# Sums of squares moved from GpSimd to TensorE, and three additions from GpSimd to VectorE, at the ends of layers

## The chip, the cores and the metric

The kernel runs on one core of a Trainium2 chip. The metric is the device time of one execution in microseconds; lower is better. Engines are named as in the profile: PE is TensorE (PEld its weight loads), DVE is VectorE, ACT is ScalarE, POOL is GpSimd, SP issues DMAs.

## The reference

The reference runs two layers of a streaming encoder on two streams, a prompt of 256 frames and 64 further frames of a running stream. The kernel handles both at once as T = 320 tokens, with D = 1024 features.

```python
for layer in range(DEPTH):                                   # DEPTH = 2
    h = rmsnorm(x, norm_mix_pre[layer])
    mix = mamba2_mixer(h, ...) if layer < N_A else mla_attend(h, ...)
    x = x + rmsnorm(mix, norm_mix_post[layer])
    f = conv_ffn(rmsnorm(x, norm_ffn_pre[layer]), ...)
    x = x + rmsnorm(f, norm_ffn_post[layer])
    if layer == N_A - 1:                                     # after the first layer
        latent, key = mla_shared_kv(x, ...)                  # starts with rmsnorm(x, kv_norm_in)
```

`rmsnorm(x, g)` is `x * rsqrt(mean(x*x) + 1e-6) * g`, the mean being over the features of a token. Four times the stream x goes through a pre-norm into a large product: at the start (Mamba input projection), at the first FFN, at the attention layer (latent, key and query projections share one sum of squares), and at the second FFN.

## The kernel before

**Layout.** x lies in SBUF as eight blocks of 128 features by 320 tokens: features on partitions, so the mean over features is a sum over partitions and over blocks. Every product with weights is done in three f32r matmuls (`mm3`): high part of the weight by high part of x (`wh`, `xgh`), `wh` by the low part `xgl`, and the weight's low part `wl` by `xgh`. ACT makes the high parts, DVE the low ones (POOL in part of the attention). Weights stream from HBM through `wr` (3 buffers) into `wh` and `wl` (4 each); an 'early' pool (`eh`, `el`) keeps a few units of the next stage.

**Scheduling.** The program is written in Python order, and a planner with its own costs sets the order on each engine; DVE and ACT between the last output block of a layer and the end of `enter` keep the written order (`self.region`). `after()` adds orderings by hand; `behind` in `outer_part` puts products behind a given PE instruction.

**End of a layer and entry of the next.** `post()` scales the eight output blocks into `y` (pool `yp`, opened by `open_y`, closed by `self.yst.close()`) and sums their squares. `late_rstd()` makes the reciprocal root of the output's mean square (`pow` on POOL, `rk`), spreads it over the partitions by PE into a PSUM tile `pr`, and returns that tile as `r`. Then `enter()` goes over the eight blocks k: `y_k *= r` (L442, DVE); `x_k += y_k` (L446, DVE, but POOL for k = 3, 5, 7); `xgh_k` (ACT, L411; for k = 0 DVE, L444); the low part `xgl` of the block before (DVE, L418 or L421); and the square of the block before (ACT, L433), which POOL adds to `xacc` (L434). At the start of the program `enter` runs with `boundary=False`, on x from the DMA.

**Products on x before its norm.** The pre-norm's root is a factor for each token, so products run on x itself (times the gain) and are scaled afterwards. `outer()` multiplies k-block by k-block into 6 PSUM tiles (4 at the start): k = 0 to 5, then `rstd_of(xacc)`, which is `toksum` (three PE matmuls of `xacc` with a column of ones, one for each 128 tokens, into a `pr` tile, L352), `mean` (DVE, `nwv`, L346) and `newton` (POOL `pow`, `rk`, L340); then k = 6 behind the sums; then `rstd_sb` (spread over partitions by PE, L359, copy by ACT to `xr`, L378); then k = 7. What follows the products (`conv` with its DVE scaling `ext`, `normalized` with `xn` on POOL) needs `xr`. In `mla()` the sums of `xacc` and of the latent's squares `kacc` go into one `pr` tile, between products k = 4 and k = 5 of the query part.

**PSUM pools.** `self.psum(**...)` closes one set of PSUM pools and opens another. Sets: `PSM = dict(m=4, x=3, r=1)` (mixer), `PSF` and `PSL = dict(m=7, r=1)` (FFN and the attention's entry), `PSA = dict(m=5, x=3)` (attention). `pr()` takes a buffer of `r` where the set has one, else of `x`.

Of the kernel before, what the change touches and what calls it, by code (L numbers as in the profile page):

```python
# [11 lines left out]
AF = mybir.ActivationFunctionType  # L12
ALU = mybir.AluOpType
# [3 lines left out]
P = 128  # L17
T = 320
TP = 256
TS = 64  # L20
D = 1024
KD = 8
NBF = 22
EPS = 1e-6
# [21 lines left out]
PSF = dict(m=7, r=1)  # L46
PSL = dict(m=7, r=1)
# [39 lines left out]
class Kern:  # L87
# [252 lines left out]
        self.nw_end = self.nc.gpsimd.tensor_tensor(out=r, in0=v, in1=self.half[:, 0:v.shape[1]], op=ALU.pow).ins  # L340
        return r

    def mean(self, src, dim, pool):

        v = self.t(pool, [P, 3], "nwv", bufs=3)
        self.nc.vector.tensor_scalar(v, src, 1.0 / dim, EPS, op0=ALU.mult, op1=ALU.add)  # L346
        return v

# [47 lines left out]
            self.high_ahead(HIGH[b])  # L396
        return ps

    def enter(self, xgp, sp, tag, g=None, boundary=True):


        nc = self.nc
        tt, act = nc.vector.tensor_tensor, nc.scalar.activation
        r = self.late_rstd() if boundary else None
        xh = self.t(xgp, [P, KD, T], "xgh", F32R, bufs=1)
        xl = self.t(xgp, [P, KD, T], "xgl", F32R, bufs=1)
        acc = self.t(sp, [P, T], "xacc", bufs=1)
        self.xhigh = []

        def high(k):  # L410
            i = act(out=xh[:, k, :], in_=self.x[:, k, :], func=AF.Copy, scale=self.v(g, k) if g and k else 1.0)  # L411
            if boundary:
                self.xhigh.append(i.ins)

        def low(k):
            h = xh[:, k, :].bitcast(F32)
            if g and k:
                i = nc.vector.scalar_tensor_tensor(out=xl[:, k, :], in0=self.x[:, k, :], scalar=self.v(g, k), in1=h,  # L418
                                                   op0=ALU.mult, op1=ALU.subtract)
            else:  # L420
                i = tt(out=xl[:, k, :], in0=self.x[:, k, :], in1=h, op=ALU.subtract)  # L421
            self.low_end = i.ins
            if boundary and k in AHEAD:
                self.gate = i.ins
                if self.lows:
                    self.lows.pop(0)()

        def square(k):
            if k == 0:
                act(out=acc, in_=self.x[:, k, :], func=AF.Square)  # L430
                return
            s = self.t(sp, [P, T], tag, bufs=2)
            act(out=s, in_=self.x[:, k, :], func=AF.Square)  # L433
            nc.gpsimd.tensor_tensor(out=acc, in0=acc, in1=s, op=ALU.add)  # L434

        with self.region if boundary else ExitStack():
            for k in range(KD + 1):
                if k < KD:
                    xk = self.x[:, k, :]
                    if boundary:  # L440
                        yk = self.y[:, k, :]
                        tt(out=yk, in0=yk, in1=r, op=ALU.mult)  # L442
                        if k == 0:
                            tt(out=xh[:, k, :], in0=xk, in1=yk, op=ALU.add)  # L444
                        e = nc.gpsimd if k in (3, 5, 7) else nc.vector
                        e.tensor_tensor(out=xk, in0=xk, in1=yk, op=ALU.add)  # L446
                        if k:
                            high(k)
                        else:
                            low(k)  # L450
                    else:
                        high(k)
                        low(k)
                if boundary and k > 1:
                    low(k - 1)
                if k:
                    square(k - 1)
        if boundary:
            self.ends.pop(0)
        return xh, xl, acc  # L460

    def normalized(self, xgp, sp, g, rstd):

# [110 lines left out]
    def outer_part(self, ps, ks, xh, xl, behind=None, turned=False):  # L574

        w = {}
        ks = list(ks)
        if ks[0] == 0:
            ks.pop(0)
            wh, wl = self.nextw()  # L580
            for j, (wt, xt) in enumerate(((wh, xh), (wl, xh), (wh, xl))):
                for b, p in enumerate(ps):
                    self.nc.tensor.matmul(p[:, :T], wt[:, b * 128:b * 128 + 128], xt[:, 0, :], start=j == 0, stop=False)
        for k, b in [(k, b) for b in range(len(ps)) for k in ks] if turned else [(k, b) for k in ks for b in range(len(ps))]:
            if k not in w:
                w[k] = self.nextw()
            s = slice(b * 128, b * 128 + 128)
            self.mm3(ps[b][:, :T], w[k][0][:, s], w[k][1][:, s], xh[:, k, :], xl[:, k, :], k == 0, k == KD - 1, behind)

    def outer(self, nblk, xh, xl, xacc, pool):  # L590

        ps = [self.pm() for _ in range(nblk)]
        a, b = OUT
        self.outer_part(ps, range(a), xh, xl)
        r = self.rstd_of(xacc, D, pool)
        self.gate = self.nw_end
        self.outer_part(ps, range(a, b), xh, xl, self.pe_end)
        r = self.rstd_sb(r, pool, "xr")
        self.outer_part(ps, range(b, KD), xh, xl, self.pe_end)
        self.xhigh = []  # L600
        return ps, r
# [96 lines left out]
    def ssm(self):  # L698
# [3 lines left out]
        with ExitStack() as st:  # L702
# [5 lines left out]
            with ExitStack() as s2:  # L708
# [4 lines left out]
                with ExitStack() as s3:  # L713
                    xtp = self.pool(s3, "xg0")
                    dp = self.pool(s3, "dtp")
                    nc.scalar.dma_start(out=self.vec[:, 0:8], in_=a["vec"][:, 0:8])
                    for k in range(KD):
                        r = self.raw[k] = self.t(dp, [P, 512], "w0", bufs=KD)
                        nc.sync.dma_start(out=r, in_=a["w_in_k"][k])
                        nc.sync.dma_start(out=self.x[:, k, :], in_=a["x"][:, k * T:(k + 1) * T])  # L720
                    nc.sync.dma_start(out=self.con, in_=a["con"][:, 0:CON["cos"][0]])
                    nc.sync.dma_start(out=self.vec[:, 8:], in_=a["vec"][:, 8:])
                    self.qd = KD
                    xh, xl, xacc = self.enter(xtp, dp, "xsq", "mix_pre0", False)
                    ps, rstd = self.outer(4, xh, xl, xacc, dp)
                    self.bt, self.ct, self.xs = {}, {}, {}
                    dt2 = self.ssm_dt(ps[0], rstd, sp, dp)
                    for i in range(1, 4):
                        self.ssm_conv(i - 1, ps[i], rstd, sp)
                    xnh, xnl, steps = self.normalized(xgp, dp, "mix_pre0", rstd)  # L730
                    szs = {0: self.t(sp, [P, 4, T], "sz", bufs=2)}
                    for i in range(3, 3 + RAW0):
                        if i == 6:
                            self.exps = self.burst = []
                            self.ssm_dt2(dt2, sp, dp)
                        p = self.block(xh, xl)
                        if i < 6:
                            self.ssm_conv(i, p, rstd, sp)
                        else:
                            nc.vector.tensor_tensor(out=szs[0][:, i - 6, :], in0=p[:, :T], in1=rstd, op=ALU.mult)  # L740
                        while len(steps) > (6, 5, 3, 1, 0)[i - 3]:
                            steps.pop(0)()
                    xh, xl = xnh, xnl
# [291 lines left out]
    def ffn(self, i):  # L1035
        nc, a = self.nc, self.a
        with ExitStack() as st:
# [3 lines left out]
            with ExitStack() as s2:  # L1041
                xgp = self.pool(s2, f"xgf{i}")
                sp = self.pool(s2, f"fs{i}")
                fsave = self.t(sp, [P, 44, 2, 2], "fsave")
                xh, xl, xacc = self.enter(xgp, sp, "xsq", f"ffn_pre{i}")
                self.yst.close()
                self.psum(**(PSF, PSL)[i])
                ps, rstd = self.outer(6, xh, xl, xacc, sp)
                self.est.close()
                self.table(AF.Gelu_apprx_tanh)  # L1050
                xnh, xnl, steps = self.normalized(xgp, sp, f"ffn_pre{i}", rstd)
# [39 lines left out]
    def mla(self):  # L1091
        nc, a = self.nc, self.a
        tt, ts, stt = nc.vector.tensor_tensor, nc.vector.tensor_scalar, nc.vector.scalar_tensor_tensor
        with ExitStack() as st:
# [10 lines left out]
            with ExitStack() as s2:  # L1105
# [3 lines left out]
                oldt = self.t(sp, [P, 2, 256], "oldt")  # L1109
                nc.sync.dma_start(out=old, in_=a["old"].rearrange("p (a b) -> p a b", a=3))  # L1110
                nc.sync.dma_start(out=oldt, in_=a["oldt"].rearrange("p (a b) -> p a b", a=2))
                xh, xl, xacc = self.enter(xgp, sp, "xsq")
                self.yst.close()
                self.psum(**PSF)
                u = self.t(kp, [P, 2, T], "u")
                kacc = self.t(sp, [P, T], "kacc")
# [16 lines left out]
                self.outer_part(ps, range(4, 5), xh, xl)  # L1133


                pt = self.pr()
                self.toksum(xacc, pt)
                self.toksum(kacc, pt, 3)
                vs = self.t(sp, [P, 6], "vs")
                ex = self.t(sp, [P, 3], "ex")  # L1140
                ts(vs[:, 0:3], pt[:, 0:3], 1.0 / D, EPS, op0=ALU.mult, op1=ALU.add)
                ts(ex, vs[:, 0:3], EPS, None, op0=ALU.mult)
                stt(out=vs[:, 3:6], in0=pt[:, 3:6], scalar=1.0 / 256, in1=ex, op0=ALU.mult, op1=ALU.add)
                self.outer_part(ps, range(5, 7), xh, xl, self.pe_end)
                rr = self.newton(vs, sp, "rr")
                r2 = self.rstd_sb(rr[:, 3:6], sp, "xk")
                xr = self.rstd_sb(rr[:, 0:3], sp, "xr", self.pm())
# [410 lines left out]
```

## Time and profile before

| | us |
|---|---|
| median of 3 runs | 983.34 (982.84 to 984.02) |
| profiled execution | 985.59 |
| its span in the trace | 983.8 |

| engine | busy us (share of the span) | instructions |
|---|---|---|
| PE | 960.0 (98%) | 6602 |
| PEld | 932.7 (95%) | 6602 |
| DVE | 738.8 (75%) | 1348 |
| ACT | 614.0 (62%) | 1247 |
| POOL | 353.5 (36%) | 560 |

The mean granted clock of PE was 0.992. How to read the rows of a timeline: start and length in us, the engine, the line of the kernel, the operation, the tile written and the tiles read, the shape; in brackets the time for which the engine stood idle before it, and what it had been waiting for. A row `x6` merges six instructions. Matmuls are pipelined and their ends are modelled, so the distance between starts is the time that a matmul takes up on PE. The four entries lie at 0 to 44 us (start), 264 to 300 (first FFN), 505 to 535 (attention) and 729 to 758 (second FFN).

### The profile page before, as it was taken

The numbers are of one execution on the slowest core, as the hardware profiler recorded it, in microseconds if no ns is written. First come the engines' busy times: TensorE is split into PE (matmuls) and PEld (weight loads), VectorE is DVE, ScalarE is ACT, GpSimd is POOL, SyncE is SP. The second block draws the span as 40 slices with busy tenths as digits, with TensorE's granted clock in tenths as the row PEclk, the third lists the DMA queues.
The fourth block names the chain that finished last, engine by engine and source line by source line (L and its number), as shares of the span: only waits on it lengthen the run. The fifth ranks groups of instructions, "written<-read, shape, count | busy, mean of one in ns | idle before, by whom it ended". The sixth has DMA issues, their size and how long they took to land.

```text
span 983.8 us, 17990 instructions
## 1 busy us (share of the span) xinstructions
PE 960.0 (98%) x6602; PEld 932.7 (95%) x6602; DVE 738.8 (75%) x1348; ACT 614.0 (62%) x1247; POOL 353.5 (36%) x560
## 2 busy tenths in 40 slices
PE   8799999999999999999999999999999999999997
PEld 8799999989989999999999899999999999999996
DVE  7989889975579998765547898885638999775432
ACT  7568988644556787654444677764645678665331
POOL 5822411000056875420017766520005777441000
PEclk9899999999999999999999999999999999999999
DMA  7465646443334545455631222233534454445541
GB/s 256 143 196 181 202 134 204 139 134 118 103 119 131 171 150 172 150 181 165 195 112 37 81 73 76 57 97 108 172 107 127 129 174 151 151 145 147 153 118 54
DMA packets 45945, 135.58 MB, mean 138 GB/s; under 512 B 5408, under 2 KB 10144, under 8 KB 45856
## 3 DMA queue, kind: packets, MB, share of 16 engines
q1 hardware_dynamic: 45712, 134.42, 43.9%
q8 instruction: 52, 0.85, 0.4%
q14 instruction: 37, 0.30, 0.1%
q10 hardware_dynamic: 144, 0.00, 0.0%
HBM read 130.29 MB, written 4.11 MB: 137 GB/s over the span
## 4 chain that ended last, share of the span: by engine, by line
PE 83%; DVE 9%; POOL 3%; ACT 2%; issue 2%; DMA 0%; SPq 0%; POOLq 0%; DVEq 0%; ACTq 0%
PE pm L284 47%; PE pm L285 23%; PE px L284 3%; PE px L285 1%; PE px L987 1%; PE px L970 1%; PE pr L352 1%; POOL xacc L434 1%; DVE wl L329 1%; PE px L978 1%; ACT wh L327 1%; POOL xn L470 1%; DVE xnl L331 1%; DVE cv L670 1%; PE px L953 1%
## 5 line engine op out<-in xcount | busy, mean ns | idle before, releaser
L329 DVE TENSOR_TENSOR wl<-wr,wh 128x1024 fp32r<-128x1024 f32 (+2 forms) x204 | 242.9, 1191 | 108.7 <-ACT wh L327 107.6
L327 ACT ACTIVATE wh<-wr 128x1024 fp32r<-128x1024 f32 (+4 forms) x235 | 227.7, 971 | 149.1 <-PE pm L284 131.5
L284 PE MATMUL pm<-xnh,wh 128*128 128x320 f32 x768 | 239.2, 312 | 0.2 <-DVE ext L660 0.2
L284 PE MATMUL pm<-xnl,wh 128*128 128x320 f32 x768 | 239.3, 312 | 0.0
L285 PE MATMUL pm<-xnh,wl 128*128 128x320 f32 x768 | 238.2, 310 | 0.0
L284 PEld LDWEIGHTS pm<-xnl,wh 128*128 128x128 f32 x768 | 144.2, 188 | 3.0 <-issue 3.0
L285 PEld LDWEIGHTS pm<-xnh,wl 128*128 128x128 f32 x768 | 144.2, 188 | 1.7 <-issue 1.7
L284 PEld LDWEIGHTS pm<-xnh,wh 128*128 128x128 f32 x768 | 144.2, 188 | 1.5 <-issue 0.7
L285 PE MATMUL pm<-ah,wl 128*128 128x320 f32 x424 | 131.3, 310 | 0.0
L284 PE MATMUL pm<-al,wh 128*128 128x320 f32 x424 | 131.2, 310 | 0.0
L284 PE MATMUL pm<-ah,wh 128*128 128x320 f32 x424 | 131.1, 310 | 0.0
L670 DVE SCALAR_TENSOR_TENSOR cv<-ext,vec,cv 128x322 f32<-128x322 f32 x176 | 98.2, 569 | 6.1 <-ACT cv L668 3.6
L664 POOL COPY fsave<-ext 128x2 f32<-128x2 f32 x88 | 71.1, 808 | 50.5 <-ACT ext L658 46.9
L340 POOL TENSOR_TENSOR rk<-nwl,half 128x3 f32<-128x3 f32 x4 | 3.4, 851 | 216.5 <-DVE nwl L391 216.5
L284 PEld LDWEIGHTS pm<-ah,wh 128*128 128x128 f32 x424 | 79.5, 188 | 1.0 <-issue 1.0
L285 PEld LDWEIGHTS pm<-ah,wl 128*128 128x128 f32 x424 | 79.6, 188 | 0.2 <-issue 0.2
L284 PEld LDWEIGHTS pm<-al,wh 128*128 128x128 f32 x424 | 79.6, 188 | 0.0
L284 PE MATMUL pm<-xgh,wh 128*128 128x320 f32 x236 | 68.6, 320 | 7.2 <-ACT xs L689 5.9
L285 PE MATMUL pm<-xgh,wl 128*128 128x320 f32 x236 | 74.2, 317 | 0.7 <-DVE wl L331 0.7
L284 PE MATMUL pm<-xgl,wh 128*128 128x320 f32 x236 | 74.1, 317 | 0.5 <-DVE xgl L418 0.5
L668 ACT ACTIVATE cv<-ext,vec 128x322 f32<-128x322 f32 x88 | 57.0, 653 | 15.1 <-POOL ext L655 9.7
L329 POOL TENSOR_TENSOR wl<-wr,wh 128x512 fp32r<-128x512 f32 (+2 forms) x31 | 43.7, 1424 | 25.2 <-ACT wh L327 22.7
(384 smaller groups left out, 2196.5 us busy)
## 6 DMA issues: line engine op xcount, KB each, us to landing
wr<-w_up SPq DMA_DIRECT2D x76, 512.0 KB, 3.3
wr<-w_in SPq DMA_DIRECT2D x37, 512.0 KB, 3.9
wr<-w_dn SPq DMA_DIRECT2D x32, 512.0 KB, 3.6
wr<-w_out SPq DMA_DIRECT2D x16, 512.0 KB, 3.4
wr<-w_o SPq DMA_DIRECT2D x16, 512.0 KB, 3.3
wr<-w_up_k SPq DMA_DIRECT2D x16, 384.0 KB, 3.4
wr<-w_dn SPq DMA_DIRECT2D x16, 384.0 KB, 3.2
dc<-acd SPq DMA_DIRECT2D x8, 512.0 KB, 6.0
```

The lines of the kernel that those rows point to most:

```text
L284: for i in (mm(out, wh, xh, start=first, stop=False), mm(out, wh, xl, start=False, stop=False), mm(out, wl, xh, start=False, stop=last)):
L285: mm(out, wl, xh, start=False, stop=last)):
L327: self.high_ins = nc.scalar.activation(out=hdst, in_=src, func=AF.Copy).ins
L329: return lambda: e.tensor_tensor(out=ldst, in0=src, in1=hdst.bitcast(F32), op=ALU.subtract)
L331: return lambda: nc.vector.scalar_tensor_tensor(out=ldst, in0=src, scalar=scale, in1=hdst.bitcast(F32), op0=ALU.mult, op1=ALU.subtract)
L352: i = self.nc.tensor.matmul(ps[:, o + b:o + b + 1], acc[:, l0:l0 + 128], self.ones[:, 0:1], start=True, stop=True)
L434: nc.gpsimd.tensor_tensor(out=acc, in0=acc, in1=s, op=ALU.add)
L470: nc.gpsimd.tensor_tensor(out=xn, in0=self.x[:, k, :], in1=rstd, op=ALU.mult)
L664: nc.gpsimd.tensor_copy(out=rows_out[:, 0, :], in_=ext[:, TP:TP + m])
L668: nc.scalar.activation(out=c, in_=ext[:, 0:n], func=AF.Identity, scale=w(0), bias=b)
L670: nc.vector.scalar_tensor_tensor(out=c, in0=ext[:, i:i + n], scalar=w(i), in1=c, op0=ALU.mult, op1=ALU.add)
L953: nc.tensor.transpose(xt_[:n, j * 128:j * 128 + 128], xs[j][:, l0:l0 + n], self.ident)
```

## The change

- `square(k)`: ACT still squares each block of x, but at an end of a layer it writes the square over the old output block `y[:, k, :]` (whose product with `r` has been added to x by then), and at the start of the program into one of eight `xsq` buffers instead of two. `xacc` and POOL's additions into it are gone.
- Each square gets a set of three PE matmuls with the column of ones (each block's set accumulates into the same three columns of one `pr` tile, `sums_tile`). The sets wait in a list, `self.sums`. `outer_part` issues the next one ahead of the weights of k while more than `KD - k + 1` are left (so block k - 2 ahead of product k); `result()`, returned by `enter` in place of `acc`, issues what is left and then `mean`.
- `outer` and `mla` call that function where they called `rstd_of(xacc)` and `toksum(xacc)`. The matmuls of the sets do not set `pe_end`, so k = 6 stands behind an older instruction than before.
- `x_k += y_k` runs on DVE for every k.
- In `ffn` and `mla`, `self.yst.close()` comes after the products instead of before them.

```diff
-    def mean(self, src, dim, pool):
+    def mean(self, src, dim, pool, v=None):
-        v = self.t(pool, [P, 3], "nwv", bufs=3)
+        v = self.t(pool, [P, 3], "nwv", bufs=3) if v is None else v
...
-    def enter(self, xgp, sp, tag, g=None, boundary=True):
+    def enter(self, xgp, sp, tag, g=None, boundary=True, mean=None):
...
-        acc = self.t(sp, [P, T], "xacc", bufs=1)
+        self.sums = []
...
         def square(k):
-            if k == 0:
-                act(out=acc, in_=self.x[:, k, :], func=AF.Square)
-                return
-            s = self.t(sp, [P, T], tag, bufs=2)
+            s = self.y[:, k, :] if boundary else self.t(sp, [P, T], tag, bufs=KD)
             act(out=s, in_=self.x[:, k, :], func=AF.Square)
-            nc.gpsimd.tensor_tensor(out=acc, in0=acc, in1=s, op=ALU.add)
+
+            def add():
+                if k == 0:
+                    self.sums_tile = self.pr()
+                sums = self.sums_tile
+                for b, l0 in enumerate(TOK):
+                    nc.tensor.matmul(sums[:, b:b + 1], s[:, l0:l0 + 128], self.ones[:, 0:1], start=k == b == 0, stop=k == KD - 1 and b == 2)
+
+            self.sums.append(add)
...
-                        e = nc.gpsimd if k in (3, 5, 7) else nc.vector
-                        e.tensor_tensor(out=xk, in0=xk, in1=yk, op=ALU.add)
+                        tt(out=xk, in0=xk, in1=yk, op=ALU.add)
...
-        return xh, xl, acc
+
+        def result():
+            while self.sums:
+                self.sums.pop(0)()
+            return self.mean(self.sums_tile[:, 0:3], D, sp, mean)
+
+        return xh, xl, result
...
             if k not in w:                                   # outer_part
+                if not turned and len(self.sums) > KD - k + 1:
+                    self.sums.pop(0)()
                 w[k] = self.nextw()
...
-    def outer(self, nblk, xh, xl, xacc, pool):
+    def outer(self, nblk, xh, xl, xv, pool):
...
-        r = self.rstd_of(xacc, D, pool)
+        r = self.newton(xv(), pool, "rk")
...                                                          # ffn
-                self.yst.close()
                 self.psum(**(PSF, PSL)[i])
-                ps, rstd = self.outer(6, xh, xl, xacc, sp)
+                ps, rstd = self.outer(6, xh, xl, xv, sp)
+                self.yst.close()
                 self.est.close()
...                                                          # mla
-                xh, xl, xacc = self.enter(xgp, sp, "xsq")
-                self.yst.close()
+                vs = self.t(sp, [P, 6], "vs")
+                xh, xl, xv = self.enter(xgp, sp, "xsq", mean=vs[:, 0:3])
                 self.psum(**PSF)
...
-                pt = self.pr()
-                self.toksum(xacc, pt)
+                xv()
+                pt = self.sums_tile
                 self.toksum(kacc, pt, 3)
-                vs = self.t(sp, [P, 6], "vs")
...
-                ts(vs[:, 0:3], pt[:, 0:3], 1.0 / D, EPS, op0=ALU.mult, op1=ALU.add)
...
                 self.outer_part(ps, range(5, 7), xh, xl, self.pe_end)
+                self.yst.close()
```

More of the change, by code (lines that the diff above doesn't have):

```diff
@@ L723, in ssm @@
                     self.qd = KD
-                    xh, xl, xacc = self.enter(xtp, dp, "xsq", "mix_pre0", False)
-                    ps, rstd = self.outer(4, xh, xl, xacc, dp)
+                    xh, xl, xv = self.enter(xtp, dp, "xsq", "mix_pre0", False)
+                    ps, rstd = self.outer(4, xh, xl, xv, dp)
                     self.bt, self.ct, self.xs = {}, {}, {}
@@ L1044, in ffn @@
                 fsave = self.t(sp, [P, 44, 2, 2], "fsave")
-                xh, xl, xacc = self.enter(xgp, sp, "xsq", f"ffn_pre{i}")
+                xh, xl, xv = self.enter(xgp, sp, "xsq", f"ffn_pre{i}")
+                self.psum(**(PSF, PSL)[i])
+                ps, rstd = self.outer(6, xh, xl, xv, sp)
                 self.yst.close()
-                self.psum(**(PSF, PSL)[i])
-                ps, rstd = self.outer(6, xh, xl, xacc, sp)
                 self.est.close()
```

## The prediction

> **What bounds the kernel now.** I read the busy times and the chain of waits first, then the busy time by stage, then the timeline of TensorE (PE) around the four places that the change touches, and last the rows of the tiles it drops.
>
> ```profile
> PE 960.0 (98%) x6602; PEld 932.7 (95%) x6602; DVE 738.8 (75%) x1348; ACT 614.0 (62%) x1247; POOL 353.5 (36%) x560
> ...
> PE 83%; DVE 9%; POOL 3%; ACT 2%; issue 2%; DMA 0%; SPq 0%; POOLq 0%; DVEq 0%; ACTq 0%
> ```
> ```profile
> 45.00:240.00 195.00, 195.00 (x1409) 182.95 (x1409) 170.03 (x286) 143.31 (x273) 37.79 (x44) 0.99 0.53 165
> 285.90:293.30 7.40, 5.45 (x25) 4.95 (x25) 3.17 (x4) 3.54 (x7) 2.94 (x3) 0.77 0.60 201
> 325.00:505.00 180.00, 180.00 (x1230) 180.00 (x1229) 129.20 (x216) 111.46 (x219) 64.88 (x143) 1.00 0.54 165
> 729.00:760.00 31.00, 30.15 (x213) 28.85 (x212) 20.68 (x37) 15.29 (x30) 13.04 (x13) 1.00 0.26 84
> 760.00:967.00 207.00, 207.00 (x1413) 207.00 (x1412) 147.20 (x252) 122.61 (x236) 81.62 (x178) 1.00 0.46 141
> ```
>
> By the second line of the page, PE makes up 83% of the chain that ends last, POOL 3%. In the rows by stage the columns are the stretch, its length, then PE, weight loads, DVE, ACT, POOL, the granted clock and the DMA. In three long stretches (582 of 983.8 us) PE is busy for every microsecond. Busy matmul time can overstate, but the products in it start every 0.15 us without a break (next fence). So outside the short holes, a microsecond of PE work that is added is a microsecond of time, and only a hole can absorb it. The second row is such a hole, with the clock down to 0.77; the fourth, the last of the four places, holds hardly any: 0.85 us idle.
>
> **What a set of three token sums costs.** Both kernels sum over partitions by f32 matmuls with a column of ones, one for each block of 128 tokens, and each is issued as two, so a set is six weight loads and six matmuls. The rows are one set among dense products, and one before k = 6:
>
> ```profile
> 263.99 0.31 PE L285 MATMUL pm<-ah,wl 128*128 128x320 f32 x1
> 264.13 0.72 PE L352 MATMUL pr<-ones,yacc 128*128 128x1 f32 x6
> 264.72 0.39 PE L284 MATMUL pm<-ah,wh 128*128 128x320 f32 x1
> 264.95 0.31 PE L284 MATMUL pm<-al,wh 128*128 128x320 f32 x1
> ```
> ```profile
> 293.35 0.72 PE L352 MATMUL pr<-ones,xacc 128*128 128x1 f32 x6
> 293.94 0.39 PE L284 MATMUL pm<-xgh,wh 128*128 128x320 f32 x1
> ```
>
> Starts are read, not durations. A set pushes the next product back by 0.59 us both times (264.72 - 264.13; 293.94 - 293.35), and the product behind it starts 0.23 instead of 0.15 us later: 0.59 for sets in a row, 0.67 for a lone one. Before, each place issues one set on the finished `xacc`; after, one set for each of eight blocks, so seven more at each of four places: 28 sets, 168 matmuls. Between 28 x 0.59 = 16.5 and 28 x 0.67 = 18.8 us I take 0.60, nearer the low end, since the last two to four sets of a place stand in a row by the order of the code, and more will if the first ones wait for the last `y` (a rival, below): 4.2 us a place, 16.8 us in all.
>
> The Trainium skill, page "TensorE: Matmul & The Clock Gate", section "Back-to-back issue gap", puts a matmul of 1 to 64 columns at about 25 ns, and its section "Step-by-step: what each phase is for" has the weight loads pulled ahead under running matmuls; by these two my estimate of a set is 6 x 25 = 150 ns, and the 28 sets would be 4.2 us instead of 16.8. The rows do not agree: 0.59 us for six is 98 ns a pair, since a matmul of one column leaves nothing to hide the next load behind.
>
> **What leaves POOL, and what comes to DVE.**
>
> ```profile
> L434 POOL TENSOR_TENSOR xacc<-xacc,xsq x28: 877/1010/1632, 7.9 to 751.7; 128x320 f32<-128x320 f32 x28
> ```
> ```profile
> L446 DVE TENSOR_TENSOR x<-x,y x15: 491/494/1164, 269.7 to 746.1; 128x320 f32<-128x320 f32 x15
> L446 POOL TENSOR_TENSOR x<-x,y x9: 1057/1124/1522, 274.6 to 748.5; 128x320 f32<-128x320 f32 x9
> ```
>
> POOL loses 28 x 1.01 + 9 x 1.12 = 38 us, but it is 36% busy, so that is worth only what waited for it. DVE gains 9 x 0.49 = 4.4 us, 1.5 at each end of a layer, hidden behind the products of the same place; without that cover, up to 1.5 us for each end. I expect the cover to hold: the same kind of addition, on DVE, takes up to 1.16 instead of 0.49 us where POOL works beside it, and that lengthening goes. The squares keep their ACT instruction and only land in `y`; `mean` is the instruction that was there; `yst.close()` later frees memory that nothing in the products uses. Each I take as 0: behind the last reader of `y` come only pools opened much later. No DMA moves; raw weight buffers come free with the low halves on DVE, at about the same time.
>
> **First layer's end (about 264 to 300 us).**
>
> ```profile
> 285.60 0.31 PE L285 MATMUL pm<-xgh,wl 128*128 128x320 f32 x1
> 287.17 0.41 PE L284 MATMUL pm<-xgh,wh 128*128 128x320 f32 x1 [1.26 <-ACT wh L330]
> 287.42 0.31 PE L284 MATMUL pm<-xgl,wh 128*128 128x320 f32 x1
> 288.41 0.64 PE L285 MATMUL pm<-xgh,wl 128*128 128x320 f32 x1 [0.69 <-DVE wl L331]
> ```
> ```profile
> 283.61 1.52 POOL L446 TENSOR_TENSOR x<-x,y 128x320 f32<-128x320 f32 x1 [0.83 <-DVE y L442]
> ```
> ```profile
> 285.17 0.56 ACT L411 ACTIVATE xgh<-x,vec 128x320 fp32r<-128x320 f32 x1 [2.16 <-POOL x L446]
> ```
>
> ACT waits 2.16 us for POOL's last addition, so its weight splits behind it come late, and PE waits. From 285.75 (the product of 285.60 plus 0.15) to the set at 293.35 PE issues the 24 products of one block in 7.60 us, at 0.15 they are 3.53: 4.07 us lost, part wait, part low clock. With x on DVE I expect it all back: 4.2 - 4.1 = +0.1. Next late would be the reciprocal root, whose last sums now stand behind the products of k = 5.
>
> **Start (0 to 44 us).**
>
> ```profile
> 17.45 0.31 PE L285 MATMUL pm<-xgh,wl 128*128 128x320 f32 x1
> 18.64 0.61 PE L352 MATMUL pr<-ones,xacc 128*128 128x1 f32 x4 [0.88 <-POOL xacc L434]
> ```
> ```profile
> 19.75 1.65 POOL L340 TENSOR_TENSOR rk<-nwv,half 128x3 f32<-128x3 f32 x1 [1.16 <-DVE nwv L346]
> ```
> ```profile
> 267.04 0.85 POOL L340 TENSOR_TENSOR rk<-nwl,half 128x3 f32<-128x3 f32 x1 [25.92 <-DVE nwl L391]
> ```
> ```profile
> 22.02 0.44 ACT L378 ACTIVATE xr<-pr 128x320 f32<-128x320 f32 x1 [3.14 <-PE pr L359]
> ```
> ```profile
> 37.53 0.31 PE L285 MATMUL pm<-xgh,wl 128*128 128x320 f32 x1
> 43.75 0.60 PE L284 MATMUL pm<-xgh,wh 128*128 128x320 f32 x1 [5.92 <-ACT xs L689]
> ```
>
> Products of k = 0 to 5 end at 17.60 and PE waits 1.04 us for POOL's sum; that goes. But eight sets must now run where one did, so the root comes 4.2 - 1.04 = 3.2 us later. Its power on POOL took 1.65 us beside DVE's splits and 0.85 elsewhere; I give that 0.8 back: +2.4. The root, spread at 22.0, then comes near 24.4. The large hole at 37.7 to 43.75 is no cover, since what ends it (normalised x, convolutions, activations) all starts from this root, so it moves along. Bounds: +4.2 (nothing back) and 2.4 - 5.9 = -3.5 (the hole closes).
>
> **Second and third ends (505 to 535, 729 to 758).**
>
> ```profile
> 530.53 0.31 PE L285 MATMUL pm<-xgh,el 128*128 128x320 f32 x1
> 530.95 0.27 PE L352 MATMUL pr<-ones,xacc 128*128 128x1 f32 x1
> ```
>
> In attention's entry PE waited only from 530.68 to 530.95: 4.2 - 0.3 = +3.9. Six of its sets now stand ahead of the latent's squares, so those come later by the same, and the chain behind them moves with PE. In the last end there was no wait for `xacc`: +4.2.
>
> **Sum.** 2.4 + 0.1 + 3.9 + 4.2 = +10.6 us. The profiled execution took 985.59 us with a span of 983.8; it would be 996.2 with a span of 994.4. The median of the runs is 983.34, 2.25 below that execution; I forecast 983.34 + 10.6 = **993.9 us**. Own range 991 to 998: the start from +0.5 to +4.2, the price of a set from 0.59 to 0.67.
>
> **Rivals.**
> *Order kept at the sums* (slower still). The sums' tile takes the one buffer `r` of a new set of PSUM pools, and both sets fill all eight banks; it can lie where the spread root lies, which DVE reads until its last `y` product:
>
> ```profile
> 275.12 1.04 PE L284 MATMUL pm<-xgh,eh 128*128 128x320 f32 x6
> ```
> ```profile
> 283.06 0.47 DVE L442 TENSOR_TENSOR y<-y,pr 128x320 f32<-128x320 f32 x1
> ```
>
> Were the first set issued as written, ahead of k = 2's products (at 275.1), PE would stand until the last `y`, about 281 with DVE relieved: some 6 us at each of two or three ends, 12 to 18 in all, 1006 to 1012. Against it: the block at 287.17 ran ahead of a set that the code has first, so issue order follows a plan that sees late inputs. 0.07.
> *Holes not given back*: the 4.07 us at the first end stay, because k = 7's split is late for another reason (its load, or DVE's extra 1.5 us): 993.9 + 4.1 = 998. 0.10.
> *Start absorbs*: the chain from the root to 43.75 is set by DVE and POOL throughput, and POOL's freedom shortens it; at most the hole's 5.9 us: 988, at half of that 991. For it POOL's 1.65 beside 0.85, against it that all of it waits for the root. 0.10.
> *Cheap sets* (faster). If loads of a set hid under products on either side, the price is what decides: 1.04 + 0.8 + 4.1 + 0.3 = 6.2 us come back, so below 6.2 / 28 = 0.22 us a set the kernel gains. At 0.15 it gives 983.34 + 4.2 - 6.2 = 981.3. Against it, both rows of a set among dense products show 0.59. 0.07.
> The forecast keeps 0.66.
>
> **Numbers.** About 0.2% (2 us) is what a measurement here can tell from no change. Faster: 0.05, most of cheap sets. Same: 0.05, its rest and the low tail of an absorbing start. Slower: 0.90. The range 987 to 999 leaves out the kept order and the cheap sets, 0.14, and a little of the tails.
>
> **What would show it.** PE count up by 168 to about 6770, its busy time up by some 14 us, and POOL's count down by 37. Around 286 to 293 no wait for ACT or DVE and a clock near 1.00. The root at the start near 24.4 instead of 22.0, and the product after the long hole near 46. In the stretch of the last end (729 to 760 now) the same work takes some 4 us more. The prediction is wrong if sets start less than 0.5 us apart, if PE waits at its first set of an end for `y`, or if the hole after 37.7 shrinks.

## The result, and the profile after

The changed kernel took 1024.3 us (median of 4 runs, 1018.63 to 1027.62) beside 983.68 us before (4 runs, 982.84 to 986.15): ratio 1.0397, 95% interval 1.0376 to 1.0419. It is 4% slower; the forecast was 993.9 us, the range 987 to 999. The profiled execution is the slowest of the four: 1027.62 us, span 1025.8.

Busy times and the chain of waits of the changed kernel:

```profile
PE 998.9 (97%) x6770; PEld 971.2 (95%) x6770; DVE 728.3 (71%) x1357; ACT 613.7 (60%) x1247; POOL 299.9 (29%) x523
...
PE 84%; DVE 8%; ACT 3%; DMA 2%; issue 1%; SPq 0%; ACTq 0%; DVEq 0%
```

PE has 168 matmuls more, as forecast, and POOL 37 instructions fewer; but PE is busy 38.9 us longer, where 14 were expected. The rows by stage (stretch, length, then PE, weight loads, DVE, ACT, POOL, granted clock, DMA) say where:

```profile
50.00:240.00 190.00, 186.25 (x1347) 172.63 (x1346) 166.78 (x283) 140.68 (x270) 31.94 (x41) 1.00 0.53 169
296.00:312.00 16.00, 16.00 (x92) 15.99 (x90) 5.50 (x12) 3.65 (x7) 2.10 (x3) 0.68 0.31 99
340.00:520.00 180.00, 180.00 (x1230) 180.00 (x1229) 127.72 (x209) 110.61 (x216) 60.36 (x140) 1.00 0.53 165
757.00:800.00 43.00, 37.13 (x243) 35.83 (x242) 18.47 (x37) 15.35 (x29) 1.75 (x2) 0.88 0.20 62
800.00:1008.00 208.00, 208.00 (x1421) 208.00 (x1420) 148.26 (x255) 122.80 (x237) 82.32 (x178) 1.00 0.45 140
```
```profile
540.00:565.00 25.00, 24.75 (x131) 24.55 (x129) 5.67 (x13) 3.73 (x8) 4.05 (x3) 0.66 0.06 19
```

The dense stretches are untouched: 180 us of the first feed-forward part hold 1230 matmuls, as before. At the three ends the granted clock is 0.68, 0.66 and 0.88, though at the first two PE is busy nearly throughout. The first end on PE's timeline (start, duration):

```profile
295.72 0.31 PE L285 MATMUL pm<-xgh,wl 128*128 128x320 f32 x1
295.86 0.31 PE L284 MATMUL pm<-xgl,wh 128*128 128x320 f32 x1
296.01 2.73 PE L437 MATMUL pr<-ones,y 128*128 128x1 f32 x24
298.61 0.39 PE L285 MATMUL pm<-xgh,wl 128*128 128x320 f32 x1
...
299.13 4.87 PE L437 MATMUL pr<-ones,y 128*128 128x1 f32 x24
303.86 0.61 PE L284 MATMUL pm<-xgh,wh 128*128 128x320 f32 x1
...
308.81 0.47 PE L284 MATMUL pm<-xgh,wh 128*128 128x320 f32 x1
309.08 0.47 PE L284 MATMUL pm<-xgl,wh 128*128 128x320 f32 x1
...
310.82 0.31 PE L285 MATMUL pm<-xgh,wl 128*128 128x320 f32 x1
310.97 0.31 PE L284 MATMUL pm<-xgh,wh 128*128 128x320 f32 x1
```

The eight sets do not stand between the products of k = 2 to 5, as the code has them, but in two runs of four sets (24 matmuls), three products apart. The first run keeps the pace of 0.65 us a set. The second, of the same shape, takes 4.73 us (303.86 - 299.13): 1.18 a set. Behind it products start 0.27 us apart (309.08 - 308.81) until 309.6, then 0.15 again. No engine is waited for; PE runs at half pace (0.27 instead of 0.15 us from product to product) for some 10 us.

The last end adds a wait. The columns are the same; the bracket is the idle time before the row and what ended it:

```profile
769.73 0.31 PE L285 MATMUL pm<-xgh,wl 128*128 128x320 f32 x1
775.05 1.41 PE L437 MATMUL pr<-ones,y 128*128 128x1 f32 x6 [5.02 <-ACT y L430]
...
779.40 0.47 PE L285 MATMUL pm<-xgh,el 128*128 128x320 f32 x1
779.67 0.47 PE L284 MATMUL pm<-xgh,eh 128*128 128x320 f32 x1
```
```profile
774.43 0.48 DVE L447 TENSOR_TENSOR y<-y,px 128x320 f32<-128x320 f32 x1
```

The first set is issued early and waits 5.02 us. The page names a square on ACT, but what ends at 774.91, just ahead, is DVE's last product of `y`, which reads the spread root in PSUM. Half pace follows until about 780.5: already this first set takes twice its time (776.32 - 775.05 = 1.27 us), with a wait ahead of it and no run of sums. It comes again after a later run of 24 matmuls.

In four parts, from the first product of the first feed-forward part, of attention's entry, of the second feed-forward part, and the span (before 269.74, 513.40, 736.01, 983.8; after 280.51, 528.85, 763.92, 1025.8):

| part | forecast | after | again | e4: one set | e2: wide sums | e6: root copied | e11: bf16 | e12: bf16 at end |
|---|---|---|---|---|---|---|---|---|
| start and mixer | +2.4 | +10.8 | +4.7 | -2.7 | +5.6 | +4.2 | -3.1 | +0.9 |
| first feed-forward (first end) | +0.1 | +4.7 | +3.1 | -4.2 | +2.3 | +1.7 | -4.6 | -4.7 |
| attention (its entry) | +3.9 | +12.5 | +10.9 | +0.1 | +6.8 | +7.3 | -0.3 | +1.9 |
| second feed-forward (last end) | +4.2 | +14.1 | +14.4 | 0.0 | +13.8 | +4.2 | +7.6 | -0.4 |
| span | +10.6 | +42.0 | +33.0 | -6.7 | +28.5 | +17.3 | -0.4 | -2.4 |

The columns behind "after" are profiles of the runs below, against the same profile of before.

### The profile page after: what moved, and what is told of

It is laid out like the page before. It is cut to its first block, busy times and chain, and to the rows that moved or that the text cites. A ratio compares the mean times of both kernels' runs of the same rounds, so it can differ in the third digit from the quotient of the medians.

```text
span 1025.8 us, 18276 instructions
## 1 busy us (share of the span) xinstructions
PE 998.9 (97%) x6770; PEld 971.2 (95%) x6770; DVE 728.3 (71%) x1357; ACT 613.7 (60%) x1247; POOL 299.9 (29%) x523
## 4 chain that ended last, share of the span: by engine, by line
PE 84%; DVE 8%; ACT 3%; DMA 2%; issue 1%; SPq 0%; ACTq 0%; DVEq 0%
PE pm L284 47%; PE pm L285 23%; PE px L284 3%; PE pr L437 3%; PE px L285 1%; DMA ea<-acd 1%; ACT wh L327 1%; DVE wl L329 1%; PE pm L593 1%; PE px L982 1%; PE px L999 1%; PE pr L352 1%; DMA wr<-w_in 1%; PE px L990 1%; DVE mx L1313 1%
## 5 line engine op out<-in xcount | busy, mean ns | idle before, releaser
L676 POOL COPY fsave<-ext 128x2 f32<-128x2 f32 x88 | 75.5, 858 | 55.9 <-ACT ext L670 50.3
L284 PE MATMUL pm<-xgh,wh 128*128 128x320 f32 x236 | 71.4, 328 | 0.9 <-DVE v L860 0.6
```

The costliest lines, as they stand in the source:

```text
L284: for i in (mm(out, wh, xh, start=first, stop=False), mm(out, wh, xl, start=False, stop=False), mm(out, wl, xh, start=False, stop=last)):
L676: nc.gpsimd.tensor_copy(out=rows_out[:, 0, :], in_=ext[:, TP:TP + m])
```

## The experiments

The theory: **a run of one-column f32 sums lowers the granted clock**, within the run and behind it. Rivals: the issue price alone, larger than thought; and waits and order alone.

**One part alone (e1), the additions of x on DVE.** In the kernel before:

```diff
-                        e = nc.gpsimd if k in (3, 5, 7) else nc.vector
-                        e.tensor_tensor(out=xk, in0=xk, in1=yk, op=ALU.add)
+                        tt(out=xk, in0=xk, in1=yk, op=ALU.add)
```


> The kernel before with one part of the change alone: all eight additions of x at an end of a layer on VectorE; the sum of squares stays on GpSimd. My theory of the first layer's end (ScalarE waits for GpSimd's last addition, the weight splits come late, PE waits) gives back its 4.07 us and nothing else: first product of attention's entry about 4 us earlier than in the kernel before (near 509.4), 979 to 980 us in all. The rival, that the stall there comes from something else late (a load, or VectorE's 1.5 us more), leaves 983 to 985. If VectorE becomes the bound at the other two ends, up to 1.5 us each come back: 986.

Measured 984.86 us, ratio 0.9995 (0.9979 to 1.0012): no change. The first end, on DVE's and PE's timelines:

```profile
283.83 1.17 DVE L445 TENSOR_TENSOR x<-x,y 128x320 f32<-128x320 f32 x1
```
```profile
287.39 0.42 PE L284 MATMUL pm<-xgh,wh 128*128 128x320 f32 x1 [1.54 <-ACT wh L330]
```

While POOL still adds squares, DVE's additions take up to 1.17 us, k = 7 stays late, PE waits 1.54 us and then runs at half pace (0.27 between products) from 289 to 295. My theory of that stall, POOL's last addition of x, was too narrow: with POOL's additions of the squares alone the stall stays.

**The 28 sets taken away (e4).** Only the eighth block's set is kept; the kernel leaves the squares of the other seven blocks out of the sum:

```diff
-            self.sums.append(add)
+            if k == KD - 1:
+                self.sums.append(add)
```


> The changed kernel with the set of the eighth block alone at each of the four places; the squares of the other seven are computed, but left out of the sum. So 28 sets are gone, as many as the kernel before has are left, and all else of the change stays (additions of x on VectorE, squares over the old output, memory freed later). If the sets are the cause, in whatever way: 976 to 980 us, that is the kernel before less the first end's 4.1 us and the 1 to 3 us of waits for GpSimd's sum. If something else in the change (memory or order) is the cause of the mixer's 10 us or of the waits at the ends, that part stays: 988 us or more.

978.87 us, ratio 0.9937 (0.9912 to 0.9962), as the theory said. The sets are the whole loss: 48.7 us between the two spans (1025.8 - 977.1), 1.74 us for each of 28; by the second execution of the changed kernel (span 1016.8) it is 39.7 us, 1.42 for each. Without them the first end gives back 4.2 us, the 4.07 of the prediction.

**Same PE time, more columns (e2).** A block is summed by one f32 product with the identity:

```diff
-                for b, l0 in enumerate(TOK):
-                    nc.tensor.matmul(sums[:, b:b + 1], s[:, l0:l0 + 128], self.ones[:, 0:1], ...)
+                nc.tensor.matmul(sums[:, 64:384], self.ident, s, start=k == 0, stop=k == KD - 1)
...
+            act(out=acc, in_=self.sums_tile[:, 64:384], func=AF.Copy)
+            self.toksum(acc, self.sums_tile)
```


> The changed kernel, but a block's square is summed by one wide f32 product with the identity (320 columns, issued as two; such pairs start 0.6 us apart in the rows of the last end, as long as a set of three one-column sums at 0.59) into 320 columns of the same bank; after the eighth one copy on ScalarE and one set of three token sums. The order of the sums on PE and what they wait for stay as in the changed kernel. Theory of the clock (a run of one-column sums halves the granted clock in the run and for some us behind it): PE's time for the sums is the same or 0.6 us a place more, but no stretch at half pace follows, so products behind the sums start 0.15 us apart, and of the 42 us some 15 to 20 go away: 1002 to 1010 us; the wait for the last product of y in the second feed-forward part stays. Theory of the issue price alone: as the changed kernel or up to 4 us slower, 1022 to 1030. Theory of waits and order alone: 1022 to 1030 too.

1013.13 us (ratio 1.0281, 1.0250 to 1.0313): 11 us of the loss gone, less than the 15 to 20 expected. The first end has the same two runs of four blocks, three products apart:

```profile
290.87 2.31 PE L436 MATMUL pr<-y,con 128*128 128x320 f32 x8
...
293.46 2.31 PE L436 MATMUL pr<-y,con 128*128 128x320 f32 x8
295.38 0.55 PE L284 MATMUL pm<-xgh,wh 128*128 128x320 f32 x1
...
296.20 0.31 PE L284 MATMUL pm<-xgl,wh 128*128 128x320 f32 x1
296.35 0.31 PE L285 MATMUL pm<-xgh,wl 128*128 128x320 f32 x1
```

A block takes 0.48 us here (1.92 for four), the sums with their last set 4.4 us a place beside 4.7; yet the second run is as fast as the first, and products go on 0.15 apart. So at this end it is the narrow matmuls, not time or order. Less came back than expected because the last end, by the table, gave back nothing (+13.8): its wait of 5.0 us stayed, and half pace followed it here too, from 761.84 to 764.9, though no narrow sum stands near. Behind the first and the last end there are also new waits for DVE, one of 0.9 and one of 0.7 us at each. Against the second execution of the changed kernel, whose start was faster, the span is only 4.5 us shorter.

**The sums set apart (e6).** One copy frees the bank that the sums need:

```diff
         r = self.late_rstd() if boundary else None
+        if boundary:
+            rc = self.t(self.yp, [P, T], "rc", bufs=1)
+            act(out=rc, in_=r, func=AF.Copy)
+            r = rc
```


> The changed kernel with one copy more on ScalarE (0.44 us) at each of the three ends: the spread root is copied from its PSUM bank to SBUF, and VectorE's eight products of y read the copy. The bank is then free for the sums at once, and by the order of instructions the sets stand 18 to 30 products apart instead of in runs. The start of the kernel is unchanged, so its 10 us until the first feed-forward part stay in every theory. Theory of the clock: lone sets cost 0.59 to 0.67 us and no half pace, so the three ends cost 4.2 - 4.1 + 0.5, 4.7 and 4.7 us, and the total is 983.7 + 10.2 + 10 = 1004 us (1000 to 1008). Theory of waits (the sums wait for the last product of y, nothing about the clock): only the 5 us wait of the second feed-forward part goes, half pace stays behind the sets: 1018 to 1020. Price alone: no change but the 0.44 us each, 1024 to 1026.

1005.34 us, ratio 1.0213 (1.0175 to 1.0251), where the theory of the clock said 1004. That the total agrees so well is partly luck: by the table the start cost 4.2 us where 10.2 were assumed, and the three ends together 13.2 where 10 were. What bears out the theory is the clock at the ends. The first sets of the first end, and the stretch of the last end:

```profile
277.52 0.72 PE L441 MATMUL pr<-ones,y 128*128 128x1 f32 x6
280.83 0.72 PE L441 MATMUL pr<-ones,y 128*128 128x1 f32 x6
```
```profile
742.00:780.00 38.00, 36.50 (x267) 35.69 (x268) 23.17 (x51) 19.64 (x38) 6.30 (x11) 1.00 0.26 84
```

Four sets stand apart, only the last four in a run; the wait is gone, the clock is 1.00, and the last part costs +4.2 us: the price forecast for it. The copy took away the wait and the longer runs together, so this run alone doesn't part the two. All 28 added sets are still there; what they cost beyond their price depended on where they stood.

**The dose (d1).** Runs of narrow matmuls among the dense products of the two down projections:

```diff
+            m = self.nc.tensor.matmul(p[:, 0:cols], self.ones, self.ones[:, 0:cols], start=True, stop=True).ins
```


> The kernel before, with runs of narrow matmuls put among the dense products of the two down projections, one run in each of six output blocks, some 9.7 us of products between two runs; each writes a PSUM bank that nobody reads. First feed-forward part: one column of ones, f32, 6, 12, 24, 48, 96 and again 6 issued matmuls (1, 2, 4, 8, 16 and 1 sets). Second: 48 issued f32 matmuls of 16, of 64 and of 128 columns, then 48 bf16 matmuls of 1, 64 and 128 columns. Theory of the clock: up to 12 matmuls (1.2 us) nothing follows; 24 (2.6 us) are enough to halve the granted clock shortly after they end, sometimes not, 48 and 96 always; behind them products start 0.27 us apart for 4 to 10 us, and within the longest run the matmuls start 0.2 instead of 0.1 us apart. With more columns in flight the drop goes: 128 columns keep the clock, 16 do not; 64 is the case to see. bf16 of one column drops it as f32 does. Theory of the issue price alone: every run costs 0.1 us a matmul and the product behind it starts 0.15 us after the one before, whatever its length. Both: 288 issued f32 sums cost some 30 us; with the clock some 20 us more.

```profile
465.41 2.73 PE L1104 MATMUL pm<-ones 128*128 128x1 f32 x24
...
477.77 7.93 PE L1104 MATMUL pm<-ones 128*128 128x1 f32 x48
485.56 0.61 PE L288 MATMUL pm<-ah,wh 128*128 128x320 f32 x1
...
940.56 6.66 PE L1104 MATMUL pm<-ones 128*128 128x16 f32 x48
...
958.74 5.47 PE L1104 MATMUL pm<-ones 128*128 128x64 f32 x48
...
988.82 1.35 PE L1102 MATMUL pm<-warm 128*128 128x1 bf16 x48
```
```profile
483.00:486.00 3.00, 3.00 (x15) 3.00 (x16) 0.46 (x1) 0.61 (x1) 0.00 (x0) 0.50 0.26 76
961.00:964.00 3.00, 3.00 (x29) 3.00 (x29) 0.11 (x1) 0.00 (x0) 0.00 (x0) 1.00 0.56 162
```

One execution, 1044.95 us. Runs of 6 and 12 leave the clock alone, and so did this one of 24. The run of 48 takes 7.9 us instead of the 4.9 that it would at 0.1 a matmul, with the clock at 0.50 from some 2 us into it, and 18 products at half pace follow; 96 take 17.5 us. With 16 columns the clock falls too, with 64 and 128 it does not. A bf16 run of one column, not foreseen so, is over too soon to tell about the clock. By its row's length it costs 0.028 us a matmul; by starts, as for the f32 sets, 0.025 (the next product starts at 990.03).

**The dose again (d2).** Six runs of 24 and six of 36 in the same places:

```diff
+DOSE = (((12, 1, 'f32'),) * 6, ((18, 1, 'f32'),) * 6)
```


> The kernel before with the same run of one-column f32 sums six times in the first down projection (24 issued matmuls, 2.6 us at full pace) and a run half as long again six times in the second (36, 3.9 us), some 9.7 us of products between two. One run of 24 kept the clock where it was tried, while runs of 24 at the ends of layers, with other sums a few us ahead of them, were followed by half pace, and a run of 48 lost it 2.1 us after its start. Theory (the clock is judged over a stretch of some us that runs on its own, so a run of this length falls into one stretch or across two): of six runs of 24 few or none lose the clock, of six of 36 some do, at different distances from their start. Rival (a fixed length decides): all six of a kind alike.

```profile
463.66 0.31 PE L287 MATMUL pm<-ah,wh 128*128 128x320 f32 x1
463.80 0.42 PE L287 MATMUL pm<-al,wh 128*128 128x320 f32 x1
464.02 0.47 PE L288 MATMUL pm<-ah,wl 128*128 128x320 f32 x1
...
467.22 0.34 PE L288 MATMUL pm<-ah,wl 128*128 128x320 f32 x1
467.40 0.31 PE L287 MATMUL pm<-ah,wh 128*128 128x320 f32 x1
```

One execution, 1052.93 us. Here the theory's "few or none" failed: all six runs of 24 were followed by half pace, as were all six of 36, so that the rival was right on whether the clock falls, though not on how long. The rows are those behind the run at 460.10, whose own 24 matmuls took 2.60 us at full pace: half pace begins 1.1 us behind it and lasts 3.4 us. Of the twelve, eight have 12 to 14 products at half pace, about 3.4 us; the other four 19 to 23, up to 6.2. So 24 in a run is at the edge: of the seven in d1 and d2 one kept the clock, and so did the two that e6 has left at its first and last end (clock 1.00 in the 7 us from the start of each).

**The changed kernel once more (again).** No edit.

> The changed kernel once more, one look, to see what of it is the same in another execution. In its first profile the products of the start ran at half pace from 4.9 to 15.9 us, with the first sums among them, though the same instructions in the same order ran at full pace there with the copied root. Theory: the start's half pace is a matter of when the clock comes up against the first run of sums, and differs from one execution to the next, by up to 5 us at the start and in the total (1018 to 1028 us in four runs); the half pace behind the sums at the three ends of layers is there each time, and so is the wait of 5.0 us in the second feed-forward part. Rival: the start is the same each time, and the spread of the times comes from the ends.

1018.64 us. The half pace at the three ends and the 5.0 us wait are there again; the start is not the same. The second set at the start, after and again, and the root at the start, after and again:

```profile
10.66 1.27 PE L437 MATMUL pr<-ones,xsq 128*128 128x1 f32 x6
```
```profile
7.95 0.72 PE L437 MATMUL pr<-ones,xsq 128*128 128x1 f32 x6
```
```profile
30.17 0.42 ACT L378 ACTIVATE xr<-pr 128x320 f32<-128x320 f32 x1
```
```profile
24.96 0.42 ACT L378 ACTIVATE xr<-pr 128x320 f32<-128x320 f32 x1
```

In the first execution the products of the start ran at half pace until 15.9 us with the sets among them, in the second at full pace; this is read from starts (0.27 us apart), for the granted clock reads 1.00 in these first 16 us. That is 5.2 us at the root and a large part of the spread of the times.

**POOL's additions on DVE, sums as before (e8, e10).** e8 at the first end alone, e10 at the start and all three ends:

```diff
-            nc.gpsimd.tensor_tensor(out=acc, in0=acc, in1=s, op=ALU.add)
+            nc.vector.tensor_tensor(out=acc, in0=acc, in1=s, op=ALU.add)
```


> The kernel before, with GpSimd taken out of the first layer's end alone: there the three additions of x and the seven of the running sum of squares are VectorE's, with one token sum as before; the other three places are as before. With x alone on VectorE the stall of 285.75 to 293.35 stayed, and there VectorE's steps still took up to 1.2 instead of 0.5 us while GpSimd added squares. Theory (GpSimd's additions beside VectorE's lengthen VectorE's steps, whichever additions they are): the stall goes, less 3.4 us that VectorE has more to do, of which products cover most: 980 to 981.5 us. Rival (VectorE then is the bound): the 3.4 us take the place of the lengthening, 983 to 986.

> The kernel before with all 37 additions of GpSimd's at the start and the three ends on VectorE (xacc and x), sums of tokens as before, one set a place. Theory of contention: the first end's stall goes, the root at the start comes 1 us earlier, the other two ends have little to win: 979 to 981 us. Rival: VectorE, 3.4 us a place longer, becomes late for the low halves at some place: 984 to 988 us.

984.24 us (1.0002, 0.9985 to 1.0019) and 989.48 us (1.0051, 1.0035 to 1.0067). Both rivals held, e10 even 1.5 us above its range: at the first end PE still waits 2.26 and 2.25 us for ACT's `wh`, though DVE's additions of x there take 0.49 us again. The 4 to 5 us of the first end came back in full only in the versions where the additions of squares left both engines (e4, e11, e12).

**Cheap sums (e11, e12).** The squares rounded to bf16, summed against a bf16 column of ones; e12 also drops the early places:

```diff
-            s = self.y[:, k, :] if boundary else self.t(sp, [P, T], tag, bufs=KD)
+            s = self.y[:, k, :].bitcast(BF16)[:, 0:T] if boundary else self.t(sp, [P, T], tag, BF16, bufs=KD)
...
-                if not turned and len(self.sums) > KD - k + 1:
-                    self.sums.pop(0)()
```


> The changed kernel with the squares written as bf16 (ScalarE rounds them) and summed against a bf16 column of ones; same sets, same order. In the run of 48 bf16 matmuls of one column among dense products they started 0.028 us apart, where f32 ones took 0.098 to 0.108 at full pace. So a place's 24 matmuls are 0.7 us instead of 48 that are 4.7, and no run reaches the 2 to 3 us behind which the clock fell. Theory of clock and price together: what is left of the change is the kernel with one set a place (978.9 us) and the 5.0 us wait for the last product of y in the second feed-forward part, 984 us (981 to 987). If waits or the order of the plan carry more than that, 990 us or more. If the 0.028 us do not hold between f32 products, 0.1 us a matmul: 990.

> As the one with bf16 sums, and none of the sets is put between the products of k = 2 to 5: all eight stand where the sum is read, so that the first set of the second feed-forward part has no early place at which it waits. Theory: the 5.0 us go too, and the time is that of the kernel with one set a place, which had one f32 set of 0.6 us where this has 0.7 us: 978 to 981 us, faster than the kernel before. Rival: the gain of the kernel with one set came from something that its missing sums made possible (the root known early, since only the last square counts): 983 us or more.

e11: 986.52 us, 1.0023 (1.0008 to 1.0038), 2.5 us above its 984. e12: 981.40 us, 0.9965 (0.9954 to 0.9976), 0.4 us above the range of its theory and the fastest version that sums all eight squares. PE's wait for the first set of the last end in e11 (us, times, longest), and all eight sets of the last end of e12:

```profile
PE pr L438 <- DVE y L448: 4.9, 1, 4.9
```
```profile
750.55 0.75 PE L438 MATMUL pr<-oneb,y 128*128 128x1 bf16 x24
```

In e11 the page names DVE's product of `y`, as the bank needs it. Behind that wait the products run at half pace, with only three bf16 sums ahead of them; the stretch from the end of the wait to full pace, in the columns of the other stretches, and the same for e2:

```profile
739.00:744.70 5.70, 5.66 (x26) 5.46 (x26) 3.73 (x6) 3.23 (x7) 0.00 (x0) 0.50 0.16 57
```
```profile
761.80:764.80 3.00, 2.96 (x9) 2.59 (x10) 1.93 (x4) 2.54 (x6) 0.00 (x0) 0.50 0.00 0
```

So the wait alone is enough to bring half pace, and in e11 the two together, 4.9 us and some 2.9 at half pace, make up the +7.6 of its last end. In e12 that wait is gone and 24 sums take 0.61 us by starts (the next product starts at 751.16).

## Why the prediction was wrong

**The failing step is the cost of a set.** It was read off two lone sets among dense products, 0.59 us, which is right where sets stand apart: +4.2 in the last part of e6. But the clock in those rows was full and the prediction priced all 28 with it, though it expected some in a row: the lower clock was no term of its sum. What is lost at half pace comes on top. Attention's entry before and after, from its first product to the first product of the query part that reads `cqh`:

```profile
513.40:537.00 23.60, 23.49 (x162) 23.21 (x163) 17.75 (x33) 10.11 (x25) 14.77 (x13) 1.00 0.13 37
```
```profile
528.85:564.80 35.95, 35.70 (x204) 35.60 (x205) 16.21 (x36) 10.31 (x25) 4.05 (x3) 0.76 0.08 24
```

At the first end 16 us at clock 0.68 lose 5.1; at attention's entry 25 us at 0.66 lose 8.5, where the same work before had the full clock. At the last end half pace from 794.4 to 797.6, behind a run of 24, costs 1.6, and half pace from 775.1 to 780.5, behind the wait, 2.7. So 15.2 us are lost behind runs of sums, nearly as much as all 28 sets were forecast to cost, and 7.7 to the wait and the half pace behind it.

The reason given for the price, that a matmul of one column leaves nothing to hide the next weight load behind, is not enough: bf16 matmuls of one column, each with a load of its own, start 0.025 us apart, and in d1 the f32 matmuls of 64 and of 128 columns start 0.11 us apart, as those of one column do in runs.

**First layer's end (+0.1 forecast, +4.7).** The stall was given back as said: DVE's 24 additions of x take 0.48 to 0.50 us, and no wait for ACT or DVE is left.

```profile
L450 DVE TENSOR_TENSOR x<-x,y x24: 483/492/495, 280.5 to 774.9; 128x320 f32<-128x320 f32 x24
```

The 5.1 us of half pace replaced it: 4.2 - 4.1 + 5.1 = 5.2. The cause given was at most half right (e1): with POOL's squares left, moving the additions of x gave back nothing. Whether taking away the squares alone would have done it was not tried.

**Attention's entry (+3.9, +12.5).** 3.9 + 8.5 of clock is 12.4, and the two rows above differ by 12.35 us. In the second execution 25 us at clock 0.73 lose 6.8, and the part costs +10.9. With the sets apart (e6) +7.3 remains: there the entry stands behind a wait of 2.06 us for DVE's `xgh` (0.35 before), and its first 24 products take 5.17 us instead of 3.63; some 2 us of it are not explained.

**Last end (+4.2, +14.1).** 4.2 + 5.0 of wait + 2.7 at half pace behind it + 1.6 behind the run is 13.5. The wait is the rival *order kept at the sums*, given 0.07: its mechanism (the sums' bank is the one that the last product of `y` reads) is what happened, at one end of three; it priced the wait, not the half pace behind it. The argument against it, that the plan moves products ahead of a set that would wait, held at the other two, but there it gathered the sets into runs, which the prediction had as harmless.

**Start (+2.4, +10.8).** The root was forecast at 24.4 and came at 24.96 in the second execution, whose mixer ended +4.7 late; in the first one half pace delayed it to 30.2. The long hole at 37.7 to 43.75 vanished, against what was written, but nothing came of it: the plan of the mixer changed and new waits of 2.2, 1.9 and 1.6 us stand later. Which of the plan's choices led to them was not tried, so the cause of this part stays open.

**Rivals.** *Holes not given back* and *start absorbs* did not decide. *Cheap sets* had a price to beat, 0.22 us a set: bf16 sets cost 0.08 (0.61 / 8), and e12 gains; but e11 has them as cheap and does not, because of the wait. Of the three signs named for a wrong forecast, two came: PE waited at the first set of an end for `y`, and the hole shrank.

## What to carry to other kernels

A price read from a row holds at the clock of that row: before adding many small matmuls, ask how long a run they make and of how few columns, and look for half pace (0.27 instead of 0.15 here) behind the runs that the trace already has. Keep narrow sums apart, make them wide, or make them short. And before moving a sum onto a PSUM bank, name the last reader of what lies there: here PE stood 5.0 us at one set, with products behind it that had not waited before, and then ran at half pace for 3 to 6 us more.

## What the runs showed of the hardware

- PE that is busy without a gap can lose its clock. f32 matmuls of 1 and of 16 columns in a run did it some 2 to 4 us after the start of the run, 64 and 128 columns in runs of 5.5 us did not. Waits lose it too: half pace followed the 5 us wait of the last end in all four versions that have it (after, again, e2, e11). The Trainium skill, page "TensorE: Matmul & The Clock Gate", section "What's actually happening", has a monitor of activity with a free-running window of about 3.4 us and a clock that is half or full; the half pace of 3.4 us behind eight of twelve runs, and a start that differs between executions, agree with it. Its section "HAM oscillation — how this bites in real kernels" warns of idle gaps longer than about 3.4 us; the waits of 5 us agree. Behind the runs of narrow f32 matmuls there was no gap, so gaps are not the only way.
- One-column matmuls, each with a weight load of its own, start 0.098 to 0.108 us apart in f32 (as issued) at the full clock, 0.025 in bf16. In f32 64 and 128 columns are no dearer: 0.11 us. The same page's section "Back-to-back issue gap" has some 25 ns for narrow ones: the bf16 run agrees, the f32 runs do not.
- POOL's additions slow DVE's beside them: the same addition of x took up to 1.17 instead of 0.49 us, also where POOL added only squares (e1).
